# Half-size raw weight buffers, a fourth split buffer and five smaller moves in a two-layer encoder on one core

## The chip, the core and the metric

The kernel runs on one core of a Trainium2 chip. The metric is the time of one execution on the device in microseconds (us); the median of the timed runs counts. The core has a matrix engine (PE, with weight loads shown apart as PEld), a vector engine (DVE), a scalar engine (ACT), a general engine (POOL) and a queue engine that issues most DMAs (SP). Weights and activations come from HBM into an on-chip memory (SBUF); PE writes its sums into PSUM.

## The reference

An encoder of four sub-layers over 256 positions with 2048 channels, all in float32. Each is preceded by an RMS norm and added to the residual; a last RMS norm ends it.

```python
for i in range(DEPTH):                 # DEPTH = 2
    hn = rms_norm(h, mix_norm[i])
    h = h + (mixer_a(hn, ...) if i % 2 == 0 else mixer_b(hn, ...))
    h = h + conv_ffn(rms_norm(h, ffn_norm[i]), w_up[i], conv_w[i], conv_b[i], w_down[i])
return rms_norm(h, final_norm)
```

- Mixer A: attention with 16 query heads on 4 key and value heads of 128 channels. q and k are RMS-normalised per head, multiplied by a gain and rotated by row and column angles.
- Mixer B: three groups of 8 heads of dilated window attention with a table of relative biases; the groups are weighted by their softmax sums.
- FFN: an up-projection to 2 x 5632 channels, a width-3 convolution over positions for each channel (three taps and a bias per channel), then `silu(gate) * value`, then a down-projection.

## The kernel before

All 256 positions stay on the chip as the residual `h`; the weights stream past. A product of two float32 matrices is made of three matmuls in a reduced format: each operand is split into a high part (a rounded copy, made by ACT) and a low part (the rest, made by DVE), and high x high, high x low and low x high are added up in PSUM (`acc`).

**Weights.** `feed` handles a chunk of 512 x 512 weights (1 MB): one buffer `raw` (tag "raw", NRAW = 3), loaded by one DMA on SP, then two halves. For each half, ACT writes `wh` (line 150) and DVE writes `wl` (line 151), both of them tags with NHL = 3 buffers; then come 12 matmuls of 512 columns (lines 138 to 140). At the start of the kernel, where the hook loads the input beside the weights, a chunk is loaded in 4 or 2 pieces. `feed_T` is the same with the weights as the stationary operand, for the FFN's up-projection: one `raw` buffer holds two groups of 512 KB, each with its own DMA, split at lines 110 and 111, with 8 matmuls of 512 columns (line 122) and 8 of 256 (line 120).

**Order.** The program is written in order of use, and a scheduler fixes each engine's order when the kernel is built. Instructions under `tc.high_priority(offset=AHEAD)`, the splits of the weights, are ranked as if they stood 45 instructions earlier. An engine works through its queue in that fixed order and waits on semaphores.

**Work between the weights.** Everything that is not a weight matmul is a generator put into `pending` by `start`. `step()`, called after each half chunk, advances the first pending generator to its next `yield`; a generator that ends hands the same step to the next one. When nothing is pending, the step goes to `spare`, which holds the bias work. `step(True)`, in the middle of a half, only goes on after a `yield "half"`.

- `qk_post` (mixer A) scales and squares a projection, multiplies by cosines (DVE, line 583) and sines (POOL, line 588), reduces the squares (line 591), takes the root (DVE, then POOL at line 267, tile `rqk`) and adds the two products (line 594, tile `ro`). PE then transposes `ro` for q (`heads_T`, line 485).
- `attend` runs over the 4 heads of a group, six steps `k`: scores and exponentials of head `k`, transposition of head `k-1` (line 653) and product with v of head `k-2` (`mm3`, lines 204 to 206). Two heads share one PSUM tile `ot`. The result is split into the slots `ah` and `al` (lines 190 and 191). Four PSUM tiles (`psp`) serve all of this.
- `late_transpose` turns the new residual into the next layer's stationary operand by DVE block transposes (line 231) at the end of each sub-layer.
- `taps`, in `ffn`, transposes the convolution's taps (`cr`, loaded on POOL at lines 314 and 315) into `cw` by three PE transposes (line 322).
- `bias_lines`, the spare work of the first FFN, expands mixer B's bias table: one small matmul per block of four heads (line 692), a copy to `ln` (six buffers), and four DMAs on POOL to DRAM (line 698), from where mixer B reads skewed windows.

Of the kernel before, what the change touches and what calls it, by code (L numbers as in the profile page):

```python
# [13 lines left out]
P = 128  # L14
# [8 lines left out]
NRAW, NHL = 3, 3  # L23
AHEAD = 45
# [4 lines left out]
def tile_encoder(ctx: ExitStack, tc: tile.TileContext, x, xT, w_a, w_ao, q_gain, k_gain, w_b, w_bo,  # L29
# [68 lines left out]
    def feed_T(acc, lhs, w, n, hh, kgs, first, last):  # L98
        raw = spool.tile([P, 4, 512], F32, tag="raw", name=nm("raw"), bufs=NRAW)
        r = raw.rearrange("p a c -> p (a c)").rearrange("p (k c) -> p k c", c=NT)  # L100
        for i, kg in enumerate(kgs):
            src = w[n, kg].rearrange("p (k c) -> p k c", c=512)[:, :, hh * NT:(hh + 1) * NT]
            nc.sync.dma_start(r[:, 4 * i:4 * i + 4, :], src)
        for i, kg in enumerate(kgs):
# [3 lines left out]
            rk = r[:, 4 * i:4 * i + 4, :]  # L108
# [16 lines left out]
    def feed(accs, lhs, kg, wap, first, last, by_m=False, pieces=1, mid=None):  # L125
        raw = spool.tile([P, 4, 512], F32, tag="raw", name=nm("raw"), bufs=NRAW)
        rawf, w = raw.rearrange("p a c -> p (a c)"), 2048 // pieces
        for i in range(pieces):
            nc.sync.dma_start(rawf[:, i * w:(i + 1) * w], wap[:, i * w:(i + 1) * w])
            if mid is not None:  # L130
                mid(i)
        def mms(order):
            for m, kt in order:
                (wh, wl), j = hls[kt // 2], kt % 2
                xh, xl = lhs[4 * kg + kt][:2]
                st, sp = first and kt == 0, last and kt == 3
                c = slice(m * P, (m + 1) * P)
                nc.tensor.matmul(accs[m], xh[:, c], wh[:, j, :], start=st, stop=False)  # L138
                nc.tensor.matmul(accs[m], xh[:, c], wl[:, j, :], start=False, stop=False)  # L139
                nc.tensor.matmul(accs[m], xl[:, c], wh[:, j, :], start=False, stop=sp)  # L140
# [152 lines left out]
    def bcast_rstd(rbc, rstd, pool, more):  # L293
# [7 lines left out]
        more()  # L301

    def ffn(l, hT, ss_in, g_next, last, side=None):
        with tc.tile_pool(name=nm("fpool"), bufs=1) as fp:
# [7 lines left out]
            cr = fp.tile([P, 3, P], F32, name=nm("cr"))  # L312
            rows = conv[l].rearrange("b o (r c) -> (b o r) c", c=P)
            nc.gpsimd.dma_start(cr[:, 0:2, :], rows[0:2 * P].rearrange("(a p) c -> p a c", p=P))
            nc.gpsimd.dma_start(cr[:NROW - 2 * P, 2, :], rows[2 * P:NROW])
            cw = fp.tile([P, NROW], F32, name=nm("cw"))

            def taps():
                t = ps_tile()
                for a in range(3):  # L320
                    w = min(P, NROW - a * P)
                    nc.tensor.transpose(t[:, a * P:a * P + w], cr[:w, a, :], ident[:w, :w])
                nc.vector.tensor_copy(cw, t[:, :NROW])

# [9 lines left out]
            start(bcast_rstd(rbc, rstd, fp, taps))  # L334
# [166 lines left out]
    def mixer_a():  # L501
        with tc.tile_pool(name="apool", bufs=1) as ap:
# [4 lines left out]
            rp = ap.tile([P, 2, 2, P], F32, name="rp")  # L507
            gbs = [ap.tile([P, P], F32, name=f"gb{i}") for i in range(2)]
# [3 lines left out]
            def tables():  # L512
                nc.sync.dma_start(rp, rope)
                for (nme, g), gb in zip((("k", k_gain), ("q", q_gain)), gbs):
# [57 lines left out]
            def qk_post(accs, which, keep, scale=1.0):  # L572
# [10 lines left out]
                nc.vector.tensor_tensor(rv, sv, ct[:, :, None, :].to_broadcast([P, 2, 4, P]), ALU.mult)  # L583
# [6 lines left out]
                yield  # L590
                nc.vector.tensor_reduce(ssq, sq.rearrange("p m (a c) -> p (m a) c", a=4), axis=AX.X, op=ALU.add)
                rsqrt_mean(r, ssq, P * scale * scale, EPS / (scale * scale))
                yield
                nc.vector.tensor_tensor(ro, ro, t2, ALU.add)
# [18 lines left out]
            v = evac_split(ap, va, rstd[0])  # L613

            def attend(g, accs):
# [9 lines left out]
                for k in range(6):  # L625
# [31 lines left out]
                    if k >= 2:  # L657
                        i = k - 2
                        pT = pTs.pop(i)
                        if i % 2 == 0:  # L660
                            ot = ps_tile()
                        j = i % 2
                        for kt in range(2):
                            mm3(ot[:, j * NT:(j + 1) * NT], v, pT,
                                (slice(None), kt, slice(g * P, (g + 1) * P)),
                                (slice(None), slice(kt * NT, (kt + 1) * NT)), kt == 0, kt == 1)
                        hi, lo = slots[4 * g + i]
                        split(hi, lo, ot[:, j * NT:(j + 1) * NT])
# [3 lines left out]
            return out_proj(w_ao, slots, kgs, 1, 1, junk, ap, "sq")  # L672
# [4 lines left out]
    def bias_lines():  # L677
        with tc.tile_pool(name="lpool", bufs=1) as lp:
# [8 lines left out]
            for b in range(6):  # L687
# [6 lines left out]
                ln = lp.tile([P, 512], F32, tag="ln", name=nm("ln"), bufs=6)  # L694
                nc.vector.tensor_copy(ln[:, :w], t[:, :w])
                dst = scr0[4 * b:4 * b + 4] if b < 2 else scr1[4 * (b - 2):4 * (b - 2) + 4]
                for i in range(4):
                    nc.gpsimd.dma_start(dst[:, 32 * i:32 * i + 32, :], ln[:, :w])

    def mixer_b(hT, ss_in):  # L700
        with tc.tile_pool(name="bpool", bufs=1) as bp:
# [24 lines left out]

            allp = slice(None)
            for hf in range(2):
# [94 lines left out]
                for g in range(3):  # L823
# [7 lines left out]
            return out_proj(w_bo, slots, [0, 2, 4, 1, 3, 5], 3, 3, junk, bp, "vl")  # L831

    hT, ss = mixer_a()
    hT, ss = ffn(0, hT, ss, 2, False, bias_lines)
    hT, ss = mixer_b(hT, ss)
    ffn(1, hT, ss, None, True)

# [83 lines left out]
```

## Time and profile before

| | |
|---|---|
| timed runs | 2304.93, 2303.80, 2304.74 us; median 2304.74 |
| profiled execution | 2306.52 us, of which the span from first to last instruction is 2304.7 |
| granted PE clock | 0.999 of full speed |
| busy | PE 2286.8 us (99%), PEld 1945.6 (84%), DVE 1635.5 (71%), ACT 1220.0 (53%), POOL 168.5 (7%) |
| DMA | 437.50 MB, mean 190 GB/s |

How to read the rows of the profile. A group has the line, engine, operation, output tile and inputs, shapes and count, then busy time in us, mean duration of one in ns, and the engine's idle time before these instructions with what ended it. A row of the waits has "engine line <- who ended the wait: us in total, times, longest us". A row of the timeline has the start in us, the duration in us, engine, line, operation, tiles, count, and in brackets the idle time before it. A row of windows has the stretch, its length, the busy time of PE, PEld, DVE, ACT and POOL with the number of instructions, the granted PE clock, the share of the DMA engines and GB/s. A row of DMA issues has tiles, queue, count, size of one and the median time from issue to landing. PE's matmuls overlap and their ends are modelled, so their starts are what to compare.

### The profile page before, as it was taken

The page shows a single profiled execution, that of the slowest core. Times are in us where ns is not written, and L with a number is a line of the kernel's source. Part 1 is how long each engine was busy: PE and PEld are TensorE (multiplying, and loading weights), DVE is VectorE, ACT ScalarE, POOL GpSimd, SP SyncE. Part 2 cuts the span into 40 slices and gives each one's busy share as a digit, 9 for nine tenths or more (in the row PEclk, how much of TensorE's full clock was granted, in tenths as well). Part 3 has the DMA queues.
Part 4 walks back from the last instruction along what each step waited for, and adds up shares of the span by engine and source line. Part 5 has one row for each costly group of instructions (what it writes and reads, how often), then busy time and mean ns, then how long its engine had stood idle before and what let it go on. Part 6 is the DMA issues. An engine that isn't in the chain of part 4 may idle for free.

```text
span 2304.7 us, 30252 instructions
## 1 busy us (share of the span) xinstructions
PE 2286.8 (99%) x11641; PEld 1945.6 (84%) x11641; DVE 1635.5 (71%) x2285; ACT 1220.0 (53%) x1746; POOL 168.5 (7%) x167
## 2 busy tenths in 40 slices
PE   9999999999999999999999999999999999999998
PEld 7888788888888888888888888878888888888886
DVE  6877876776457776778876876576777754677755
ACT  6565565655345555445454454445556543555543
POOL 2331001200000000010000000000000000000010
PEclk9999999999999999999999999999999999999999
DMA  8434566755555555565555554556655555555654
GB/s 301 164 129 157 184 202 192 239 191 186 198 192 192 185 190 193 184 221 197 197 169 183 171 194 164 180 186 208 195 185 191 193 188 196 190 193 184 197 187 146
DMA packets 230337, 437.50 MB, mean 190 GB/s; under 512 B 13760, under 2 KB 194752, under 8 KB 202416
## 3 DMA queue, kind: packets, MB, share of 16 engines
q1 hardware_dynamic: 223808, 425.63, 55.0%
q0 software_dynamic: 5952, 9.38, 1.7%
q8 instruction: 91, 1.49, 0.3%
q10 hardware_dynamic: 432, 0.56, 0.1%
q14 instruction: 54, 0.44, 0.1%
HBM read 429.20 MB, written 6.29 MB: 189 GB/s over the span
## 4 chain that ended last, share of the span: by engine, by line
PE 90%; DVE 6%; DMA 1%; issue 1%; ACT 1%; SPq 0%; POOLq 0%; POOL 0%; DVEq 0%; ACTq 0%
PE acc L122 27%; PE acc L139 15%; PE acc L140 15%; PE acc L138 15%; PE acc L120 14%; DVE wl L151 2%; DVE tT L231 2%; DMA raw<-in_w_up_dram 1%; PE ps L202 1%; PE ps L204 0%; PE ps L205 0%; PE ps L206 0%; DVE h L285 0%; DMA xt<-in_xT_dram 0%; PE ps L799 0%
## 5 line engine op out<-in xcount | busy, mean ns | idle before, releaser
L151 DVE TENSOR_TENSOR wl<-raw,wh 128x1024 fp32r<-128x1024 f32 (+1 forms) x456 | 555.3, 1219 | 333.5 <-ACT wh L150 330.0
L150 ACT ACTIVATE wh<-raw 128x1024 fp32r<-128x1024 f32 (+1 forms) x456 | 475.3, 1045 | 527.1 <-PE acc L140 491.7
L122 PE MATMUL acc<-xh,wh 128*128 128x512 f32 x2816 | 675.3, 391 | 0.0
L122 PEld LDWEIGHTS acc<-xh,wh 128*128 128x128 f32 x2816 | 517.1, 188 | 101.0 <-issue 1.0
L111 DVE TENSOR_TENSOR wl<-raw,wh 128x1024 fp32r<-128x1024 f32 x352 | 457.9, 1301 | 192.2 <-ACT wh L110 191.9
L110 ACT ACTIVATE wh<-raw 128x1024 fp32r<-128x1024 f32 x352 | 372.5, 1059 | 211.8 <-PE acc L122 98.7
L139 PE MATMUL acc<-wl,ah 128*128 128x512 f32 x1024 | 400.0, 391 | 2.5 <-DVE wl L151 2.2
L138 PE MATMUL acc<-wh,ah 128*128 128x512 f32 x1024 | 399.2, 390 | 0.0
L140 PE MATMUL acc<-wh,al 128*128 128x512 f32 x1024 | 398.6, 389 | 0.0
L120 PEld LDWEIGHTS acc<-xh,wl 128*128 128x128 f32 x2816 | 361.6, 191 | 16.2 <-DVE wl L111 2.2
L120 PE MATMUL acc<-xh,wl 128*128 128x256 f32 x2816 | 366.6, 283 | 1.8 <-DVE wl L111 1.8
L138 PE MATMUL acc<-wh,xh 128*128 128x512 f32 x768 | 302.5, 395 | 0.3 <-ACT wh L150 0.2
L139 PE MATMUL acc<-wl,xh 128*128 128x512 f32 x768 | 299.8, 390 | 0.5 <-DVE wl L151 0.5
L140 PE MATMUL acc<-wh,xh 128*128 128x512 f32 x768 | 299.3, 390 | 0.0
L139 PEld LDWEIGHTS acc<-wl,ah 128*128 128x128 f32 x1024 | 192.2, 188 | 46.7 <-DVE wl L151 7.6
L138 PEld LDWEIGHTS acc<-wh,ah 128*128 128x128 f32 x1024 | 192.2, 188 | 39.8
L140 PEld LDWEIGHTS acc<-wh,al 128*128 128x128 f32 x1024 | 192.2, 188 | 39.6
L140 PEld LDWEIGHTS acc<-wh,xh 128*128 128x128 f32 x768 | 144.1, 188 | 30.2
L139 PEld LDWEIGHTS acc<-wl,xh 128*128 128x128 f32 x768 | 144.5, 188 | 29.3 <-DVE wl L151 1.7
L138 PEld LDWEIGHTS acc<-wh,xh 128*128 128x128 f32 x768 | 144.3, 188 | 28.6 <-ACT wh L150 1.2
L366 POOL TENSOR_TENSOR cv<-cg,cv 128x512 f32<-128x512 f32 x44 | 63.0, 1431 | 1137.8 <-DVE cv L358 1137.8
L346 ACT ACTIVATE v<-acc 128x256 f32<-128x256 f32 x176 | 66.4, 377 | 111.1 <-PE acc L122 111.1
(152 smaller groups left out, 1386.2 us busy)
## 6 DMA issues: line engine op xcount, KB each, us to landing
raw<-in_w_up_dram SPq DMA_DIRECT2D x352, 512.0 KB, 5.0
raw<-in_w_down_dram SPq DMA_DIRECT2D x88, 1024.0 KB, 4.8
raw<-in_w_b_dram SPq DMA_DIRECT2D x72, 1024.0 KB, 4.8
raw<-in_w_bo_dram SPq DMA_DIRECT2D x24, 1024.0 KB, 4.8
raw<-in_w_a_dram SPq DMA_DIRECT2D x16, 1024.0 KB, 4.8
raw<-in_w_ao_dram SPq DMA_DIRECT2D x16, 1024.0 KB, 4.8
raw<-in_w_a_dram SPq DMA_DIRECT2D x16, 256.0 KB, 5.8
raw<-in_w_a_dram SPq DMA_DIRECT2D x8, 512.0 KB, 8.7
```

The lines of the kernel that those rows point to most:

```text
L110: nc.scalar.activation(wh, rk, AF.Copy)
L111: nc.vector.tensor_tensor(wl, rk, wh.bitcast(F32), ALU.subtract)
L120: nc.tensor.matmul(acc[j][:, :NT], wl[:, kt, c], lhs[4 * kg + kt][0], start=st, stop=sp)
L122: nc.tensor.matmul(acc[j], wh[:, kt, c], lhs[4 * kg + kt][2], start=st, stop=sp)
L138: nc.tensor.matmul(accs[m], xh[:, c], wh[:, j, :], start=st, stop=False)
L139: nc.tensor.matmul(accs[m], xh[:, c], wl[:, j, :], start=False, stop=False)
L140: nc.tensor.matmul(accs[m], xl[:, c], wh[:, j, :], start=False, stop=sp)
L150: nc.scalar.activation(wh[:, c], r[:, c], AF.Copy)
L151: nc.vector.tensor_tensor(wl[:, c], r[:, c], wh[:, c].bitcast(F32), ALU.subtract)
L231: nc.vector.transpose(o[cols].rearrange("p a (m t) -> p a m t", m=2)[:, :, :, rows], s[rows].rearrange("p m (a c) -> p a m c", c=P)[:, :, ...
L346: nc.scalar.activation(v[:, j], acc[j][:, NT:], AF.Copy)
L366: nc.gpsimd.tensor_tensor(cv, cg, cv, ALU.mult)
```

## The change

- NRAW and NHL go from 3 to 4, AHEAD from 45 to 60. A `raw` buffer now holds half a chunk, so each half has its own buffer. In `feed` a chunk that one DMA of 1 MB loaded is loaded by two of 512 KB; in `feed_T` the two DMAs stay as they are.
- `load_taps` takes the loading and transposing of the taps out of `ffn`: mixer A calls it behind its v projection, mixer B at its start, and the transposes become a generator in the mixer's steps. `cr` and `cw` lie in the pool of the weights.
- `qk_post`: the product with the cosines moves one step later; the reduction and the root move behind the addition.
- `attend`: each head has its own PSUM tile for the product with v.
- `bias_lines`: a `yield` stands before each of the four DMAs, and `ln` has two buffers.
- The rotary tables `rp` and `gbs` share the buffers of the transposed probabilities, `pTh` and `pTl`.

```diff
-NRAW, NHL = 3, 3
-AHEAD = 45
+NRAW, NHL = 4, 4
+AHEAD = 60
...
     def feed_T(acc, lhs, w, n, hh, kgs, first, last):
-        raw = spool.tile([P, 4, 512], F32, tag="raw", name=nm("raw"), bufs=NRAW)
-        r = raw.rearrange("p a c -> p (a c)").rearrange("p (k c) -> p k c", c=NT)
-        for i, kg in enumerate(kgs):
+        raws = []
+        for kg in kgs:
+            raw = spool.tile([P, 2, 512], F32, tag="raw", name=nm("raw"), bufs=NRAW)
+            raws.append(raw.rearrange("p a c -> p (a c)").rearrange("p (k c) -> p k c", c=NT))
             src = w[n, kg].rearrange("p (k c) -> p k c", c=512)[:, :, hh * NT:(hh + 1) * NT]
-            nc.sync.dma_start(r[:, 4 * i:4 * i + 4, :], src)
+            nc.sync.dma_start(raws[-1], src)
...
     def feed(accs, lhs, kg, wap, first, last, by_m=False, pieces=1, mid=None):
-        raw = spool.tile([P, 4, 512], F32, tag="raw", name=nm("raw"), bufs=NRAW)
-        rawf, w = raw.rearrange("p a c -> p (a c)"), 2048 // pieces
-        for i in range(pieces):
-            nc.sync.dma_start(rawf[:, i * w:(i + 1) * w], wap[:, i * w:(i + 1) * w])
+        raws, w = [], 2048 // pieces
+        for i in range(max(pieces, 2)):
+            if pieces < 4 or i % 2 == 0:
+                raws.append(spool.tile([P, 2, 512], F32, tag="raw", name=nm("raw"), bufs=NRAW))
+            w = min(w, 1024)
+            r = raws[-1].rearrange("p a c -> p (a c)")
+            k = i % 2 if pieces == 4 else 0
+            nc.sync.dma_start(r[:, k * w:(k + 1) * w], wap[:, i * w:(i + 1) * w])
             if mid is not None:
                 mid(i)
...
-            r = raw[:, 2 * s:2 * s + 2, :]
+            r = raws[s]
...
+    def load_taps(l):
+        cr = spool.tile([P, 3, P], F32, tag="cr", name=nm("cr"), bufs=1)
+        cw = spool.tile([P, NROW], F32, tag="cw", name=nm("cw"), bufs=1)
+        rows = conv[l].rearrange("b o (r c) -> (b o r) c", c=P)
+        nc.gpsimd.dma_start(cr[:, 0:2, :], rows[0:2 * P].rearrange("(a p) c -> p a c", p=P))
+        nc.gpsimd.dma_start(cr[:NROW - 2 * P, 2, :], rows[2 * P:NROW])
+
+        def turn():
+            yield
+            t = ps_tile()
+            for a in range(3):
+                w = min(P, NROW - a * P)
+                nc.tensor.transpose(t[:, a * P:a * P + w], cr[:w, a, :], ident[:w, :w])
+            nc.vector.tensor_copy(cw, t[:, :NROW])
+
+        return cw, turn()
...
-            rp = ap.tile([P, 2, 2, P], F32, name="rp")
-            gbs = [ap.tile([P, P], F32, name=f"gb{i}") for i in range(2)]
+            rp = ap.tile([P, 2, 2, P], F32, tag="pTh", name="rp", bufs=2)
+            gbs = ap.tile([P, 4, P], F32, tag="pTl", name="gbs", bufs=2)
...
             def qk_post(accs, which, keep, scale=1.0):
...
-                nc.vector.tensor_tensor(rv, sv, ct[:, :, None, :].to_broadcast([P, 2, 4, P]), ALU.mult)
...
                 yield
+                nc.vector.tensor_tensor(rv, sv, ct[:, :, None, :].to_broadcast([P, 2, 4, P]), ALU.mult)
+                yield
+                nc.vector.tensor_tensor(ro, ro, t2, ALU.add)
                 nc.vector.tensor_reduce(ssq, sq.rearrange("p m (a c) -> p (m a) c", a=4), axis=AX.X, op=ALU.add)
                 rsqrt_mean(r, ssq, P * scale * scale, EPS / (scale * scale))
-                yield
-                nc.vector.tensor_tensor(ro, ro, t2, ALU.add)
...
             v = evac_split(ap, va, rstd[0])
+            cw, turn = load_taps(0)
+            start(turn)
...
-                        if i % 2 == 0:
-                            ot = ps_tile()
-                        j = i % 2
+                        ot = ps_tile()[:, :NT]
...
-                ln = lp.tile([P, 512], F32, tag="ln", name=nm("ln"), bufs=6)
+                ln = lp.tile([P, 512], F32, tag="ln", name=nm("ln"), bufs=2)
...
                 for i in range(4):
+                    yield
                     nc.gpsimd.dma_start(dst[:, 32 * i:32 * i + 32, :], ln[:, :w])
...
     def mixer_b(hT, ss_in):
...
+            cw, turn = load_taps(1)
...
+                if hf == 0:
+                    start(turn)
                 for g in range(3):
                     start(v_gen(g, project(w_b, 6 * g + 4 + hf, hT, kgs)))
```

More of the change, by code (lines that the diff above doesn't have):

```diff
@@ L291, in junk_of, with bcast_rstd @@
         return lambda: pool.tile([P, 512], F32, tag="junk", name=nm("junk"))
-    def bcast_rstd(rbc, rstd, pool, more):
+    def bcast_rstd(rbc, rstd, pool):
         dg = pool.tile([P, 2, P], F32, name=nm("dg"))
@@ L300, in bcast_rstd, with ffn @@
         nc.vector.tensor_copy(rbc, t[:, :NT])
-        more()
-    def ffn(l, hT, ss_in, g_next, last, side=None):
+    def load_taps(l):
[12 more added lines that the diff above has]
+        return cw, turn()
+    def ffn(l, hT, ss_in, cw, g_next, last, side=None):
         with tc.tile_pool(name=nm("fpool"), bufs=1) as fp:
@@ L311, in ffn @@
                 nc.gpsimd.dma_start(fin, final_norm.partition_broadcast(P))
[L312 to L323, printed above, removed]
             def tap(n, j, i):
@@ L333, in ffn @@
             rb4 = rbc.rearrange("p (m t) -> p m t", m=2)[:, None].to_broadcast([P, 2, 2, P])
-            start(bcast_rstd(rbc, rstd, fp, taps))
+            start(bcast_rstd(rbc, rstd, fp))
             def halves(v):
@@ L513, in tables @@
                 nc.sync.dma_start(rp, rope)
-                for (nme, g), gb in zip((("k", k_gain), ("q", q_gain)), gbs):
+                for i, (nme, g) in enumerate((("k", k_gain), ("q", q_gain))):
+                    gb = gbs[:, i, :]
                     nc.sync.dma_start(gb, g.partition_broadcast(P))
```

19 lines of the change are left out of this document (9 added, 10 removed).

## The prediction

> **What bounds the kernel now.** I read the page first, then the waits of PE's weight loads over the whole run, then the timelines of PE, DVE and ACT around each wait found there.
>
> ```profile
> span 2304.7 us, 30252 instructions
> PE 2286.8 (99%) x11641; PEld 1945.6 (84%) x11641; DVE 1635.5 (71%) x2285; ACT 1220.0 (53%) x1746; POOL 168.5 (7%) x167
> PEld acc L139 <- DVE wl L151: 9.2, 15, 0.9
> PEld ps L204 <- DVE al L191: 2.8, 3, 0.9
> PEld acc L120 <- DVE wl L111: 2.2, 1, 2.2
> PEld ps L485 <- DVE ro L594: 1.4, 1, 1.4
> ```
>
> PE is busy 99% of the span and nearly always has its operands. The change removes no large matmul, so it can only win back the moments at which PE stood still. These are few: 15 waits for the low half `wl` of a split weight in `feed`, 3 for a low half `al` in mixer A, 1 for `wl` in `feed_T`, 1 for the rotated query `ro`. The change touches each of them. A microsecond taken out of PE's stream comes off the end, since no other engine is near its limit (DVE 71%).
>
> PEld's idle time overstates a stall, because a load normally runs ahead of its matmul. The loss is the spacing of matmul starts against the steady one:
>
> ```profile
> 257.30 0.39 PE L140 MATMUL acc<-wh,al 128*128 128x512 f32 x1
> 257.52 0.39 PE L138 MATMUL acc<-wh,ah 128*128 128x512 f32 x1
> 258.42 0.50 PE L139 MATMUL acc<-wl,ah 128*128 128x512 f32 x1 [0.51 <-DVE wl L151]
> 258.76 0.40 PE L140 MATMUL acc<-wh,al 128*128 128x512 f32 x1
> ```
>
> Steady spacing is 0.23 us (257.30 to 257.52; over long stretches 0.227). Here it is 0.90 and then 0.34, so the wait cost 0.67 + 0.11 = 0.78 us, 0.15 less than the 0.93 us that PEld idled. I take 0.15 off each PEld wait. A half chunk of `feed` is 12 such matmuls, 12 x 0.227 = 2.72 us; that is the beat of the kernel.
>
> **Fourth split buffer and AHEAD.** Where do the 15 waits lie? The same view in three stretches (230 to 270, 960 to 1000, 1500 to 1520 us), which are the ends of mixer A, of the first FFN and of mixer B, and DVE's timeline in the first:
>
> ```profile
> PEld acc L139 <- DVE wl L151: 3.7, 6, 0.9
> PEld acc L139 <- DVE wl L151: 1.8, 3, 0.8
> PEld acc L139 <- DVE wl L151: 2.0, 3, 0.9
> 254.88 2.23 DVE L231 STREAM_TRANSPOSE tT<-h 32x256 f32<-32x256 f32 x5
> 257.14 1.23 DVE L151 TENSOR_TENSOR wl<-raw,wh 128x1024 fp32r<-128x1024 f32 x1
> 230.00:270.00 40.00, 38.80 (x167) 30.22 (x167) 38.17 (x63) 21.35 (x33) 0.00 (x0) 1.00 0.48 162
> ```
>
> Twelve waits, 7.5 us less 12 x 0.15, so 5.7 us of PE time. The cause is seen in DVE: five block transposes of the next layer's input stand before each split, 2.23 + 1.23 = 3.46 us of DVE work to a beat of 2.72, so DVE falls 0.7 us behind with each half until the block is done. Over the whole stretch it keeps up (38.17 us of 40). With three buffers a `wh` may be written once PE has finished the half three back; with four, one beat (2.72 us) earlier. The stretches lose 2.8 (in two groups 15 us apart), 1.35 and 1.55 us, each less than the beat gained. I count 5.2 of the 5.7 us, bounds 3.0 (DVE's fixed order puts some split still later) and 5.7. The other three waits (1.7 us of PEld, 1.25 after the deduction) lie in the first 20 us, where data, not buffers, are late: 0, at best 1.25.
>
> **Raw half chunks.** The four half-size buffers hold four halves where three whole ones held six, but a half is now freed by its own `wl` and not by its partner's.
>
> ```profile
> raw<-in_w_up_dram SPq DMA_DIRECT2D x352, 512.0 KB, 5.0
> raw<-in_w_down_dram SPq DMA_DIRECT2D x88, 1024.0 KB, 4.8
> raw<-in_w_a_dram SPq DMA_DIRECT2D x8, 512.0 KB, 8.7
> L151 DVE TENSOR_TENSOR wl<-raw,wh 128x1024 fp32r<-128x1024 f32 (+1 forms) x456 | 555.3, 1219 | 333.5 <-ACT wh L150 330.0
> L150 ACT ACTIVATE wh<-raw 128x1024 fp32r<-128x1024 f32 (+1 forms) x456 | 475.3, 1045 | 527.1 <-PE acc L140 491.7
> 800.00:810.00 10.00, 10.00 (x61) 8.92 (x60) 6.71 (x11) 5.77 (x8) 0.00 (x0) 1.00 0.66 208
> ```
>
> A slot's round is landing + `wh` + `wl` = 5.0 + 1.05 + 1.22 = 7.3 us against 4 beats = 10.9 us, so 3.6 us hide the smaller store. Each 1024 KB transfer becomes two of 512 KB; on SP only weights stand behind them. No trace has such a half transfer in this place: the nearest rows are 5.0 us (same size, 1 KB rows) and 8.7 us (same rows as the new ones, but in the first 40 us, where the queues are full). Cost 0 at 5.0; a round at 8.7 is 10.97 us, just the limit.
>
> The Trainium skill ("DMA: Bandwidth & Descriptors", section Bandwidth) says to batch transfers to 1 MiB or more for 75% of peak, which speaks against halving them. Its formula in the section on the anatomy of one DMA (2.0 us + bytes / 436 GB/s, given for GpSimd's path) makes 3.2 us of 512 KB, an estimate, more than a beat if they came one at a time. The trace disagrees: the last row is a stretch of `feed_T`, which already lives on 512 KB transfers, and PE is busy 10.00 of 10.00 us at 208 GB/s.
>
> At the start the store matters, because the fourth chunk's pieces are issued early:
>
> ```profile
> 11.71 2.59 SPq L129 DMA_DIRECT2D raw<-in_w_a_dram  x4
> 14.48 1.28 DVE L151 TENSOR_TENSOR wl<-raw,wh 128x512 fp32r<-128x512 f32 x2
> 15.00:20.00 5.00, 4.73 (x21) 3.62 (x20) 4.49 (x8) 4.59 (x9) 0.00 (x0) 1.00 1.03 401
> ```
>
> They will have to wait for the second chunk's splits, the last of which ends at 15.8, so up to 2.5 us later, with the loads of x and the rotary tables behind them on SP. But the DMA engines are full there (share 1.03): a transfer that joins a full queue later, in the same order, lands hardly later. Bounds 0 and +1.5, I take +0.6.
>
> **PSUM tile per head.**
>
> ```profile
> 108.62 0.39 PE L139 MATMUL acc<-wl,xh 128*128 128x512 f32 x1
> 109.53 0.39 PE L204 MATMUL ps<-pTh,vh 128*128 128x256 f32 x1 [0.52 <-DVE al L191]
> 109.76 0.28 PE L205 MATMUL ps<-pTl,vh 128*128 128x256 f32 x1
> 109.88 0.28 PE L206 MATMUL ps<-pTh,vl 128*128 128x256 f32 x1
> 108.47 0.68 DVE L191 TENSOR_TENSOR pTl<-ps,pTh 128x512 fp32r<-128x512 f32 x1
> 109.07 0.41 DVE L191 TENSOR_TENSOR al<-ps,ah 128x256 fp32r<-128x256 f32 x1
> ```
>
> The fourth head's product waits for `al` of the third, which is read from the other half of the same tile. Loss 0.91 - 0.23, and 0.23 - 0.12 after it: 0.79 us, in three of the four groups, 2.4 us. With a tile of its own the product can start at 108.85. Next late is `pTl` (done at 109.15), which its second matmul needs at 108.97: up to 0.35 us stays if DVE's queue is as before, so at least 1.3 us is won; DVE has less before it (next part), so I take 2.2. A step now takes three of the four tiles, and a score tile gets the slot of a product two steps older, some 5 us: free, and 0.8 us a time where that cover fails.
>
> **Rotary of q and k.**
>
> ```profile
> 81.27 0.39 PE L140 MATMUL acc<-wh,xh 128*128 128x512 f32 x1
> 82.68 1.09 PE L485 MATMUL ps<-ident,ro 128*128 128x128 f32 x8 [1.02 <-DVE ro L594]
> 80.29 1.20 DVE L591 TENSOR_REDUCE ssq<-sq 128x8 f32<-128x1024 f32 x1
> 81.42 1.21 DVE L594 TENSOR_TENSOR ro<-ro,t 128x1024 f32<-128x1024 f32 x1
> 53.08 2.56 POOL L267 TENSOR_TENSOR rqk<-ms,nhalf 128x8 f32<-128x8 f32 x1 [1.82 <-DVE ms L266]
> ```
>
> PE lost 1.41 - 0.23 = 1.18 us here. With the reduction behind the addition, `ro` ends 1.2 us earlier, at about 81.5, when PE wants it. The multiplication by the cosines moves one beat later, in front of it; I take 1.0, bounds 0 and 1.2. The root `rqk` for q starts when it does now, since reduction and addition only change places. For k the root comes up to one beat and one reduction (1.20) later, 3.9 us, and DVE would stand before the product with it, at worst for all of that, with the splits behind it. The fourth buffer covers 2.72 of the 3.9 us: 0.2 lost, bounds 0 and 1.2.
>
> **Bias copies.**
>
> ```profile
> 402.11 0.59 PE L692 MATMUL ps<-oh,lh 128*128 128x256 f32 x2
> 404.46 1.21 PE L120 MATMUL acc<-xh,wl 128*128 128x256 f32 x8 [1.76 <-DVE wl L111]
> raw<-in_w_up_dram SPq DMA_DIRECT2D x10, 512.0 KB, 11.4
> scr<-ln POOLq DMA_DIRECT2D x8, 256.0 KB, 16.8
> ```
>
> The last two rows are the transfers between 376 and 410 us: copies of four at a time, up to 1 MB, and beside them weights that need 11.4 instead of 5.0 us. PE pays once: the starts of L692 and L120 are 2.35 us apart, of which the row counts 1.76 as idle; some 2.0 us can go. One copy per spare step (some five spare steps in eight `feed_T` beats of 2.8 us, one in 4.4 us) adds 58 GB/s instead of a burst, so I take 1.9, bounds 1.0 (some delay stays) and 2.0. `ln` with two buffers waits for copies eight or more spare steps old, 35 us against the 16.8 us of landing: free.
>
> **Taps, tables in other tiles.** The three transposes and one copy are moved, not removed; PE does not wait at the old place nor need it at the new one; the two small transfers go ahead on POOL, busy 7%. 0.
>
> **Sum.** 5.2 + 2.2 + 1.0 + 1.9 - 0.6 - 0.2 = 9.5 us. The profiled execution took 2306.52 us (span 2304.7 and 1.8 around it), so 2297.0 for such a one; the median of the three timed runs is 2304.74, 0.08% less, and the forecast is 2304.7 - 9.5 = 2295.2. All bounds at their best: 5.7 + 1.25 + 2.4 + 1.2 + 2.0 = 12.6, 2292.2. All at their worst: 3.0 + 1.3 + 0 + 1.0 - 1.5 - 1.2 = 2.6, 2302.1.
>
> **Rivals.**
> A. *The fourth buffer does not help*: the order of DVE's queue is fixed, and transposes keep their places before the splits. Against: DVE has 1.8 us in 40 to spare, and each loss is under a beat. For: a longer AHEAD moves the order in ways that this trace cannot show. Without its 5.2 us: 2300.4.
> B. *Slower: splits in front of evacuations.* ACT works in order and already spends 491.7 us in front of a `wh`, waiting for PE. If the fourth buffer and the longer AHEAD put one more `wh` ahead of the exponentials and evacuations of mixer A, then PE waits for these at a price like that of `al`, 0.79. At all 32 places (16 heads, transposition and product) 25 us: 2304.7 - 9.5 + 25 = 2320. It turns the sign from 12 places on. Against: the waits end with the same PE events as now.
> C. *Slower: half transfers too slow.* Should a half take 9.6 us (two transfers of 4.8 one behind the other), a round is 11.9 us, 0.24 us per half over the beat: for the 176 halves of `w_down` alone 42 us, 2337. It begins at 8.6 us of landing. The batching rule of the Trainium skill ("DMA: Bandwidth & Descriptors", section Bandwidth) would lead here. `feed_T` speaks against it.
> D. *Given back in the rotary*: if DVE stands 1.5 us before the root in k and in each of four q groups with the splits behind it, 7.5 us return: 2302.7.
>
> **Chances.** Forecast 0.70, A 0.10, D 0.08, B 0.08, C 0.04. The measurement can tell 0.2%, 4.6 us, from no change: faster means under 2300.1. The forecast is faster but for its worst corner (0.68), A is on the line (0.05 each side), D is the same, B and C slower: 0.73, 0.15, 0.12. A range of 2292 to 2303 holds the forecast, A and D.
>
> **What would show it.** Right: PEld's waits for `wl` of `feed` fall from 15 to the few of the first 20 us; those for `al`, for `wl` of `feed_T` and for `ro` vanish; PE stays at 99%; landing of the 512 KB halves under 8 us. Wrong: PE waits on `wh` with a DMA as releaser (C), on `pTh` or `ah` in mixer A (B), on `wl` at the same three stretches (A), or DVE idles before L607 or L636 with POOL as releaser (D).

## The result and the profile after

| | before | after |
|---|---|---|
| median of 8 timed runs (lowest to highest), us | 2304.73 (2303.80 to 2305.41) | 2298.35 (2297.71 to 2299.45) |
| profiled execution, us (span) | 2306.52 (2304.7) | 2298.31 (2296.5) |

The ratio is 0.9971, with a 95% interval of 0.9962 to 0.998: the change makes the kernel faster by 6.4 us, 0.28%. The forecast was 2295.2 us, range 2292 to 2303. The time alone does not decide for the forecast: it is 3.2 us from it and 2.1 us from the 2300.4 of rival A, both of which the range holds. Note the profiled execution of before: it lies 1.8 us above the median of its kind, while that of after lies on its median. That difference matters below.

Span and busy times from the page of the kernel after:

```profile
span 2296.5 us, 31097 instructions
PE 2283.0 (99%) x11641; PEld 1947.3 (85%) x11641; DVE 1633.6 (71%) x2285; ACT 1218.4 (53%) x1746; POOL 164.7 (7%) x167
```

Those of PEld's waits over the whole run that bear on the change, after (L144 was L138 before, L145 was L139, L121 was L120, L123 was L122, L494 was L485):

```profile
PEld acc L123 <- DVE v L356: 1.9, 3, 1.4
PEld acc L144 <- ACT wh L156: 1.6, 1, 1.6
PEld ps L494 <- DVE ro L602: 1.0, 1, 1.0
PEld acc L145 <- DVE wl L157: 0.8, 2, 0.5
PEld acc L121 <- DVE wl L112: 0.7, 2, 0.4
```

Of the 15 waits for `wl` of `feed` 2 are left, both in the first 20 us; the three stretches at the ends of the sub-layers have none left. The waits for `al` are gone, and no `pTl` came in their place. `ro` is waited for 1.0 instead of 1.4 us. The wait for `wh` at the start is 1.6 us once, where before had 1.2 us in two. The wait for `v` (L356), an evacuation in the FFN, is new.

The spacing of PE's starts turns this into time:

| place | lost before, us | lost after, us |
|---|---|---|
| `wl` at the three sub-layer ends | 2.82 + 1.35 + 1.57 = 5.74 | 0 |
| `al`, three groups | 3 x 0.79 = 2.36 | 0 |
| `ro` at 81 us | 1.18 | 0.75 |
| bias work near 402 us | 2.0 in the profiled execution | 0 |
| first 20 us | 4.0 | 4.0 |
| start of the first FFN, 279 to 288 us | 0 | 2.2 |

Without the bias row that is 5.74 + 2.36 + 0.43 - 2.2 = 6.3 us, the 6.4 of the medians.

The last row of the table is what the prediction did not have. After, DVE's timeline at the first FFN's start, and those of DVE and PE some 9 us later:

```profile
270.45 0.48 DVE L302 TENSOR_SCALAR dg<-ident,rstd 128x128 f32<-128x128 f32 x2 [0.61 <-POOL rstd L273]
276.65 0.56 DVE L695 COPY lh<-rb 128x768 f32<-128x768 f32 x1 [5.71 <-DMA rb<-in_rel_bias_dram]
```

```profile
285.91 0.42 DVE L356 TENSOR_TENSOR v<-acc,v 128x256 f32<-128x256 f32 x1
286.38 1.23 DVE L112 TENSOR_TENSOR wl<-raw,wh 128x1024 fp32r<-128x1024 f32 x1
287.52 0.75 DVE L356 TENSOR_TENSOR v<-acc,v 128x256 f32<-128x256 f32 x2
284.54 2.34 PE L123 MATMUL acc<-xh,wh 128*128 128x512 f32 x9
287.99 1.88 PE L123 MATMUL acc<-xh,wh 128*128 128x512 f32 x7 [1.11 <-DVE v L356]
```

`lh` belongs to the spare bias work and is not wanted before the bias blocks near 370 us. Its copy stands in DVE's queue, waiting for a load `rb` of 3 KB, and for 5.71 us nothing passes it: the splits and `v` are late, and PE pays 0.37 us and some tenths from 279 us on, then 1.38 + 0.11 at 286.4. Before, the same copy, which ran only 0.65 us later, cost nothing, since two splits and an `xh` were queued ahead of it:

```profile
272.80 1.22 DVE L111 TENSOR_TENSOR wl<-raw,wh 128x1024 fp32r<-128x1024 f32 x1
274.22 1.23 DVE L111 TENSOR_TENSOR wl<-raw,wh 128x1024 fp32r<-128x1024 f32 x1 [0.20 <-ACT wh L110]
275.36 0.48 DVE L197 SCALAR_TENSOR_TENSOR xh<-ps,gain,xh 128x256 fp32r<-128x256 f32 x1
277.30 0.56 DVE L686 COPY lh<-rb 128x768 f32<-128x768 f32 x1 [1.46 <-DMA rb<-in_rel_bias_dram]
```

The landing of the weights after, on which rival C of the prediction turns:

```profile
raw<-in_w_up_dram SPq DMA_DIRECT2D x352, 512.0 KB, 3.8
raw<-in_w_down_dram SPq DMA_DIRECT2D x176, 512.0 KB, 3.7
```

### The profile page after: what moved, and what is told of

The parts are those of the page before. It is cut to its first block, busy times and chain, and to the rows that moved or that the text cites. A ratio compares the mean times of both kernels' runs of the same rounds, so it can differ in the third digit from the quotient of the medians.

```text
span 2296.5 us, 31097 instructions
## 1 busy us (share of the span) xinstructions
PE 2283.0 (99%) x11641; PEld 1947.3 (85%) x11641; DVE 1633.6 (71%) x2285; ACT 1218.4 (53%) x1746; POOL 164.7 (7%) x167
## 3 DMA queue, kind: packets, MB, share of 16 engines
q8 instruction: 91, 1.49, 0.3%
## 4 chain that ended last, share of the span: by engine, by line
PE 94%; DVE 3%; issue 1%; DMA 1%; POOL 0%; ACT 0%; SPq 0%; POOLq 0%; DVEq 0%; ACTq 0%
PE acc L123 27%; PE acc L145 16%; PE acc L144 16%; PE acc L146 16%; PE acc L121 14%; DVE tT L237 1%; DVE wl L157 1%; PE ps L208 1%; PE ps L211 1%; PE ps L210 0%; PE ps L212 0%; DMA raw<-in_w_a_dram 0%; PE ps L665 0%; PE ps L810 0%; DMA rb<-in_rel_bias_dram 0%
## 5 line engine op out<-in xcount | busy, mean ns | idle before, releaser
L123 PE MATMUL acc<-xh,wh 128*128 128x512 f32 x2816 | 675.5, 391 | 1.1 <-DVE v L356 1.1
L123 PEld LDWEIGHTS acc<-xh,wh 128*128 128x128 f32 x2816 | 517.1, 188 | 102.1 <-DVE v L356 1.9
L144 PE MATMUL acc<-wh,ah 128*128 128x512 f32 x1024 | 399.1, 390 | 0.0
L145 PE MATMUL acc<-wl,ah 128*128 128x512 f32 x1024 | 398.5, 389 | 0.0
L121 PEld LDWEIGHTS acc<-xh,wl 128*128 128x128 f32 x2816 | 361.9, 191 | 15.4 <-DVE wl L112 0.7
L121 PE MATMUL acc<-xh,wl 128*128 128x256 f32 x2816 | 367.8, 283 | 0.2 <-DVE wl L112 0.2
L144 PE MATMUL acc<-wh,xh 128*128 128x512 f32 x768 | 302.5, 395 | 1.2 <-ACT wh L156 1.2
L145 PE MATMUL acc<-wl,xh 128*128 128x512 f32 x768 | 299.9, 391 | 0.2 <-DVE wl L157 0.2
L144 PEld LDWEIGHTS acc<-wh,ah 128*128 128x128 f32 x1024 | 192.3, 188 | 39.3
L145 PEld LDWEIGHTS acc<-wl,ah 128*128 128x128 f32 x1024 | 192.2, 188 | 39.2
L144 PEld LDWEIGHTS acc<-wh,xh 128*128 128x128 f32 x768 | 144.4, 188 | 29.4 <-ACT wh L156 1.6
L145 PEld LDWEIGHTS acc<-wl,xh 128*128 128x128 f32 x768 | 144.3, 188 | 27.9 <-DVE wl L157 0.8
```

The source lines that it names most:

```text
L121: nc.tensor.matmul(acc[j][:, :NT], wl[:, kt, c], lhs[4 * kg + kt][0], start=st, stop=sp)
L123: nc.tensor.matmul(acc[j], wh[:, kt, c], lhs[4 * kg + kt][2], start=st, stop=sp)
```

## Experiments

Each time below stands beside the kernel before on the same chip: 2304.48 us for p_buffers, p_heads, p_bias and f_lh, 2304.52 for p_bufheads, p_buftaps, u_nhl3 and f_lhrot, 2304.27 for p_half, p_rot, u_ahead45 and f_lhrotlate.

### One part of the change at a time

**p_buffers**: before, with the buffers and AHEAD alone.

```diff
-NRAW, NHL = 3, 3
-AHEAD = 45
+NRAW, NHL = 4, 4
+AHEAD = 60
...
```

(`feed` and `feed_T` are those of the change.)

> The kernel before with the half-size raw buffers, the fourth split buffer and AHEAD 60 alone. Theory (each stall is its own and the gains add): the twelve waits for wl at the three sub-layer ends go, 5.7 us, so 2299.0 against 2304.7; PEld's waits for wl of feed fall from 15 to the 3 of the start; the waits for al (3), ro (1) and the bias stall of feed_T stay. Rival (the gain of the whole change comes from the small edits, and halved transfers cost what the buffers win): 2303 to 2306.

2301.47 us (2300.00 to 2304.54), ratio 0.9985 [0.9976, 0.9993]. The `wl` waits at the sub-layer ends are gone, but only 3.0 us are won, since a new wait took 3.7 back. PEld's two longest waits:

```profile
PEld ps L210 <- DVE al L197: 3.1, 3, 1.1
PEld ps L328 <- DMA cr<-in_conv_dram: 2.8, 3, 1.3
```

PE's timeline at the second of them:

```profile
274.17 0.44 PE L328 MATMUL ps<-ident,cr 128*128 128x128 f32 x2 [0.89 <-DMA cr<-in_conv_dram]
275.48 0.30 PE L328 MATMUL ps<-ident,cr 96*128 96x96 f32 x1 [0.87 <-DMA cr<-in_conv_dram]
```

Two windows behind it, in which the column after the five engines is the granted clock:

```profile
274.50:278.00 3.50, 2.63 (x14) 2.23 (x14) 0.58 (x2) 0.84 (x2) 0.00 (x0) 0.82 0.97 339
278.00:282.00 4.00, 4.00 (x15) 3.20 (x15) 3.67 (x8) 1.42 (x2) 0.00 (x0) 0.73 0.54 172
```

With PE earlier at the FFN's start, the taps `cr` come too late for their transposes: 1.15 + 1.04 us. Then the granted clock falls (0.82 and 0.73 of full speed in the windows): eight matmuls follow at up to 0.43 instead of 0.23 us, 1.5 us more.

The wait for `ro`, which was expected to stay, is gone too, although the rotary steps are those of before. DVE's timeline:

```profile
80.00 1.22 DVE L600 TENSOR_TENSOR ro<-ro,t 128x1024 f32<-128x1024 f32 x1
```

The addition ends at 81.2 us, in time for PE; before it ended at 82.6. With these 1.2 us the sum closes: 5.7 + 1.2 - 3.7 = 3.2. The half-size buffers alone do not do it, since p_half below keeps the wait.

**p_heads**: before, with a PSUM tile per head alone.

```diff
-                        if i % 2 == 0:
-                            ot = ps_tile()
+                        ot = ps_tile()[:, :NT]
```

> The kernel before with a PSUM tile per head alone. Theory: the three waits for al go whole, 2.4 us, 2302.3. Rival (pTl is next late, the rotary work still stands before it on DVE): PE waits at the second matmul of the fourth head, 1.3 us gained, 2303.4, and three waits for pTl appear at L205.

2304.07 us, ratio 1.0 [0.9991, 1.0009]: nothing. PE's timeline and DVE's in the first of the three groups:

```profile
108.09 0.28 PE L204 MATMUL ps<-pTh,vh 128*128 128x256 f32 x1
108.89 0.38 PE L205 MATMUL ps<-pTl,vh 128*128 128x256 f32 x1 [0.53 <-DVE pTl L191]
106.89 1.34 DVE L151 TENSOR_TENSOR wl<-raw,wh 128x1024 fp32r<-128x1024 f32 x1
108.16 0.68 DVE L191 TENSOR_TENSOR pTl<-ps,pTh 128x512 fp32r<-128x512 f32 x1
```

The product now starts at once and stops one matmul later, for `pTl`: 0.80 - 0.12 + 0.10 = 0.78 us, as much as `al` had cost. `pTl` stands behind a split. And PE's own order has changed: 12 matmuls of `acc` stand between this product and the one before it, where before there were 14. So PE reaches the product 0.45 us earlier, and the 0.35 us that the prediction left at `pTl` become 0.8.

**p_bias**: before, with the bias copies alone.

```diff
-ln = lp.tile([P, 512], F32, tag="ln", name=nm("ln"), bufs=6)
+ln = lp.tile([P, 512], F32, tag="ln", name=nm("ln"), bufs=2)
...
                 for i in range(4):
+                    yield
                     nc.gpsimd.dma_start(dst[:, 32 * i:32 * i + 32, :], ln[:, :w])
```

> The kernel before with one bias copy per spare step and two ln buffers alone. Theory: the 2.0 us stall of feed_T near 402 us is in every execution, so 2302.7. Rival (that stall was a feature of the one profiled execution, which at 2306.5 was 1.8 us above the median of the timed runs): 2304.4 to 2304.9, though the profile shows no such stall.

2304.18 us, ratio 0.9997 [0.9988, 1.0006]. The stall at 402 us is not in its profile, but the time is that of before. Nor is it in the profiles of p_heads (span 2302.3), p_rot, p_buffers, p_bufheads and p_buftaps, all of which have the bias copies of before. So the 2.0 us belonged to the one execution of before that was profiled, the one 1.8 us above the median.

**p_rot**: before, with the rotary steps alone.

```diff
-                nc.vector.tensor_tensor(rv, sv, ct[:, :, None, :].to_broadcast([P, 2, 4, P]), ALU.mult)
...
                 yield
-                nc.vector.tensor_reduce(ssq, ...)
-                rsqrt_mean(r, ssq, ...)
+                nc.vector.tensor_tensor(rv, sv, ct[:, :, None, :].to_broadcast([P, 2, 4, P]), ALU.mult)
                 yield
                 nc.vector.tensor_tensor(ro, ro, t2, ALU.add)
+                nc.vector.tensor_reduce(ssq, ...)
+                rsqrt_mean(r, ssq, ...)
```

> The kernel before with the rotary steps alone: the cosine product one step later, the addition in the third step ahead of the reduction. Theory of the prediction: the addition ends 1.2 us earlier, the wait of 1.18 us at 81 us goes, and the later root of k costs 0.2 to 1.2 with only three split buffers: 2303.7, bounds 2303.3 to 2304.7. Rival: it changes the order on DVE in the query groups as well, so that the product or the split of a score stands behind a split or an addition there, three times or more, 2306 or over.

2304.14 us, ratio 1.0 [0.9991, 1.0009]. PEld's waits between 60 and 100 us:

```profile
PEld acc L139 <- DVE wl L151: 0.8, 1, 0.8
PEld ps L485 <- DVE ro L592: 0.3, 1, 0.3
```

DVE's timeline:

```profile
80.72 1.21 DVE L592 TENSOR_TENSOR ro<-ro,t 128x1024 f32<-128x1024 f32 x1
81.86 1.20 DVE L593 TENSOR_REDUCE ssq<-sq 128x8 f32<-128x1024 f32 x1
```

Here the addition does stand ahead of the reduction, and the stall of 1.18 us is gone. For k a wait for a split at 70.3 us gives 0.58 + 0.11 = 0.69 us back, inside the prediction's bound of 0 to 1.2. Another 0.26 us is lost at 86 us, where the scores wait for `qTl`. The loss in k is of the kind of rival D, work of `qk_post` that holds up the splits, but DVE does not stand before the root: it stands 0.63 us before the addition, waiting for POOL's product `t`:

```profile
51.00 1.23 DVE L592 TENSOR_TENSOR ro<-ro,t 128x1024 f32<-128x1024 f32 x1 [0.63 <-POOL t L587]
```

**p_half**: before, with half-size raw buffers alone.

```diff
-NRAW, NHL = 3, 3
+NRAW, NHL = 4, 3
...
```

(`feed` and `feed_T` are those of the change; AHEAD stays 45.)

> The kernel before with half-size raw buffers (four of 512 KB in place of three of 1 MB), three split buffers and AHEAD 45 left as they are. Theory: the smaller store is hidden (a slot's round of 3.7 + 1.05 + 1.22 = 6.0 us against four beats, 10.9 us), so 2304.5 us within 2 us, the twelve wl waits at the sub-layer ends still there. Rival: the half transfers cost time by themselves, part of what the changed kernel with three split buffers lost (17.9 us over the changed kernel, 11.7 over the one before): then 2308 to 2316, with PE waiting for wh or wl with a DMA behind it.

2307.14 us (2305.41 to 2312.31), ratio 1.0014 [1.0005, 1.0023]: slower by 2.9 us, where I expected nothing within 2. The profiled execution (2306.41 us) has the stalls of before, with PE's loss 1.3 us larger than in that of p_bias: 0.5 us of it at `ro`, 0.4 near 397 us, 0.2 for the taps of the second FFN. The rest of the 2.9 us was not located.

### Parts together

**p_bufheads**: p_buffers and p_heads in one.

```diff
-NRAW, NHL = 3, 3
-AHEAD = 45
+NRAW, NHL = 4, 4
+AHEAD = 60
...
-                        if i % 2 == 0:
-                            ot = ps_tile()
+                        ot = ps_tile()[:, :NT]
```

> The kernel before with the buffers (half-size raw, fourth split, AHEAD 60) and the PSUM tile per head. Theory: the tile per head alone only changed what PE waits for (from al to pTl, which stands behind a split on DVE); with the fourth buffer pTl is ordered one split earlier, so together they win the 2.4 us that neither wins alone: 2299.1 against the 2301.5 of the buffers alone, no wait for al nor pTl. Rival (the rotary edit is what cleared DVE): PE waits for pTl three times as before, 2301.5.

2297.19 us (2296.58 to 2299.52), ratio 0.997 [0.9959, 0.9981]. PEld's waits for `cr` and `wl`:

```profile
PEld ps L328 <- DMA cr<-in_conv_dram: 3.4, 3, 1.7
PEld acc L145 <- DVE wl L157: 2.0, 4, 0.6
```

Neither `al` nor `pTl` is there. The PSUM tile, worth nothing alone, takes 4.3 us off p_buffers by the medians (whose runs spread over 4.5 us) and 2.3 us between the two profiled spans (2300.0, 2297.7); the stalls for `al` that it removes from p_buffers come to 2.7. The reason stands in DVE's timeline, where `pTl` is now ahead of the split, as it already is in p_buffers:

```profile
106.08 0.68 DVE L197 TENSOR_TENSOR pTl<-ps,pTh 128x512 fp32r<-128x512 f32 x1
106.67 1.43 DVE L157 TENSOR_TENSOR wl<-raw,wh 128x1024 fp32r<-128x1024 f32 x1
```

The profiled execution here is the slowest of its seven, 2.3 us above the median, and holds the wait for `cr` and a slow clock behind it, so that this wait need not be in every execution.

These two parts alone are 7.3 us under before, the whole change 6.4, and the intervals overlap. That the other parts of the change (rotary steps, taps, tables, bias copies) win anything on top of them is not shown.

**p_buftaps**: p_buffers with the taps loaded and transposed in the mixers, and the tables in the buffers of `pTh` and `pTl`, without which it does not fit into SBUF.

```diff
+            cw, turn = load_taps(0)
+            start(turn)
...
-            rp = ap.tile([P, 2, 2, P], F32, name="rp")
+            rp = ap.tile([P, 2, 2, P], F32, tag="pTh", name="rp", bufs=2)
...
```

> The kernel before with the buffers, the taps made in the mixers and the rotary tables in other tiles (without which it doesn't fit into the memory). Theory: with the buffers alone PE came to the taps' transposes before their data and lost 2.2 us of waiting and 1.6 us at half clock; with the taps made ready earlier this 3.8 us goes, but DVE's wait for the small bias table takes 2.3 us in its place: 2299.5 to 2300 against 2301.5. Rival (the wait for the taps was a matter of one execution): 2301.5 or more.

2300.56 us (2299.63 to 2302.57), ratio 0.998 [0.9972, 0.9989]. The wait for `cr` and the slow clock behind it (3.7 us) are gone; only 0.9 us of it shows in the medians and 2.1 in the profiled spans (2300.0, 2297.9). Part came back at the same place: `lh` now stands in DVE's queue without splits ahead of it, as DVE's timeline shows, and PE loses 1.4 us at 287.6.

```profile
277.78 0.56 DVE L698 COPY lh<-rb 128x768 f32<-128x768 f32 x1 [4.86 <-DMA rb<-in_rel_bias_dram]
```

### After with one thing changed

**f_lh**: the copy of `lh` on POOL instead of DVE.

```diff
-            nc.vector.tensor_copy(lh, rb[:, :, None].to_broadcast([P, 24, 32]))
+            nc.gpsimd.tensor_copy(lh, rb[:, :, None].to_broadcast([P, 24, 32]))
```

> The changed kernel with the copy of the bias table into lh moved from DVE to POOL. Theory: DVE's 5.7 us wait for a 3 KB transfer at the start of the first FFN is what makes PE stand for some 2.3 us between 279 and 288 us; both go, 2296.0 against 2298.35. Rival (these stalls come from the four half-size raw buffers, which hold less in front of feed_T): DVE's wait goes, PE's stalls stay, 2298.3.

2296.78 us (2295.87 to 2297.40), ratio 0.9963 [0.995, 0.9975]: 7.7 us under before, against 6.4 for after. In its profile the stalls of 279 to 288 us are gone, and its span is 2.4 us shorter than that of after (2294.1, 2296.5). Of that the medians show 1.3, with overlapping intervals; the profiled execution is 0.9 us below its median.

**u_nhl3**: three split buffers.

```diff
-NRAW, NHL = 4, 4
+NRAW, NHL = 4, 3
```

> The changed kernel with three split buffers instead of four, all else as changed. Theory (the fourth buffer, not the half-size raw ones, removes the twelve waits for wl): the waits come back, 5.7 us, and pTl stands behind a split again, 2.4 us: about 2306. Rival (half-size raw buffers and AHEAD do it): 2298 to 2299.

2316.22 us (2314.23 to 2318.15), ratio 1.005 [1.0038, 1.0063]: 11.7 us slower than before, 18 slower than after. The `wl` waits are back (8.4 us in 14); that explains the expected part. The rest lies in mixer A. The timelines of DVE and PE there:

```profile
108.27 1.23 DVE L602 TENSOR_TENSOR ro<-ro,t 128x1024 f32<-128x1024 f32 x1 [2.03 <-POOL t L597]
109.41 1.22 DVE L157 TENSOR_TENSOR wl<-raw,wh 128x1024 fp32r<-128x1024 f32 x1
110.55 0.69 DVE L197 TENSOR_TENSOR pTl<-ps,pTh 128x512 fp32r<-128x512 f32 x1
108.48 0.28 PE L210 MATMUL ps<-pTh,vh 128*128 128x256 f32 x1
111.29 0.39 PE L211 MATMUL ps<-pTl,vh 128*128 128x256 f32 x1 [2.53 <-DVE pTl L197]
```

Three windows, one behind each such stall:

```profile
112.20:115.60 3.40, 3.40 (x9) 2.65 (x8) 2.13 (x5) 1.32 (x2) 1.16 (x1) 0.50 0.79 241
146.35:149.70 3.35, 3.35 (x11) 2.87 (x12) 2.88 (x5) 0.38 (x1) 0.00 (x0) 0.50 0.89 215
182.00:186.00 4.00, 4.00 (x19) 3.20 (x19) 3.40 (x6) 1.44 (x2) 1.64 (x1) 1.00 0.69 232
```

The number of buffers has changed DVE's order. The addition `ro`, which nobody wants for a long while, stands ahead of `pTl` and waits 2.03 us for POOL's product (in after `pTl` starts at 106.95 and the addition at 110.71); PE waits for `pTl` 2.7 us in each of three groups. After two of them the clock is granted at half (0.50) for 3.4 us and costs another 1.6 us each time. These are 11.3 us; with the 5.7 of the `wl` waits, 17.0 of the 18.

**u_ahead45**: AHEAD back at 45, four buffers kept.

```diff
-AHEAD = 60
+AHEAD = 45
```

> The changed kernel with AHEAD 45 instead of 60, four split buffers kept. Theory: the gain at the sub-layer ends is the buffer's and not the longer priority offset's, so no wl waits come back at 240 to 270, 968 to 995 and 1509 to 1516 us: 2298.3 within 1.5 us; the two kernels differ mainly in where reductions and splits stand on DVE in mixer A, which may move the wait for ro by 0.5 us. Rival: the offset carries part of it, wl waits of 2 us or more come back, 2300.5 or over.

2295.80 us (2295.26 to 2297.23), ratio 0.9963 [0.995, 0.9976]: 8.5 us under before. No `wl` wait comes back at the sub-layer ends, so the gain there is the buffer's. Against after the longer AHEAD costs 2.1 us (6.4 and 8.5 under their befores). DVE's timeline at two places:

```profile
78.46 1.33 DVE L157 TENSOR_TENSOR wl<-raw,wh 128x1024 fp32r<-128x1024 f32 x1
79.71 1.21 DVE L602 TENSOR_TENSOR ro<-ro,t 128x1024 f32<-128x1024 f32 x1
276.83 0.56 DVE L695 COPY lh<-rb 128x768 f32<-128x768 f32 x1 [6.04 <-DMA rb<-in_rel_bias_dram]
286.05 0.75 DVE L356 TENSOR_TENSOR v<-acc,v 128x256 f32<-128x256 f32 x2
```

One split stands ahead of `ro` instead of two, and `ro` is in time; `lh` waits as long as ever, but the two pieces of `v` follow each other without a split between them, and PE does not stop there. That is 0.75 + 1.38 = 2.1 us, what the medians say. The profiled spans differ by only 1.0 us (2296.5, 2295.5): the profiled execution of u_ahead45 is the slowest of its five, 1.4 us above the median, and loses 0.7 us more than that of after in the first 20 us.

**f_lhrot**: `lh` on POOL, and the addition raised by 20 places.

```diff
+                with tc.high_priority(offset=20):
-                nc.vector.tensor_tensor(ro, ro, t2, ALU.add)
+                    nc.vector.tensor_tensor(ro, ro, t2, ALU.add)
```

> The changed kernel with lh copied on POOL and the rotary addition ranked 20 places earlier, so that it stands between two splits and behind the reduction. Theory: the addition can begin when POOL ends the sine products, some 1.0 us earlier for the first group, so the 0.75 us that PE still loses before the first q transposes goes: 2296.0 against the 2296.8 with lh alone. Rival (DVE then waits for POOL in front of a split, and in the later groups in front of pTl): 2296.8 to 2299, with waits for wl or pTl in mixer A.

2295.25 us (2294.89 to 2295.70), ratio 0.996 [0.9947, 0.9972]: 9.3 us under before, the lowest of all, though u_ahead45 is within its interval. The stall at 81 us is gone; DVE's timeline shows the addition starting as soon as POOL's product `t` allows:

```profile
80.11 1.23 DVE L603 TENSOR_TENSOR ro<-ro,t 128x1024 f32<-128x1024 f32 x1 [0.64 <-POOL t L597]
```

**f_lhrotlate**: the same, with the taps' loads held back until `v` exists.

```diff
-            cw, turn = load_taps(0)
+            cw, turn = load_taps(0, v[0][:, 0, 0:1].bitcast(F32))
...
-    def load_taps(l):
+    def load_taps(l, after=None):
...
+        if after is not None:
+            for a in (0, 2):
+                nc.gpsimd.tensor_copy(cr[:, a, 0:1], after)
```

> The changed kernel with lh copied on POOL, the rotary addition put ahead of the reduction, and the taps' two loads for the first FFN held back until v exists, so that they and their three transposes no longer stand in the first 10 us. Theory: the start loses the wait for wh near 7 us (0.7 to 1.4 us in the profiles of the changed kernel and of the version without the hold), so 0.5 to 1.0 us under that version's 2295.25: 2294.5. Rival: the start waits for x and the weights, which arrive when they arrive, and the taps (180 KB) are no part of it: 2295.3 within 0.4.

2296.48 us (2296.03 to 2297.76), ratio 0.9966 [0.9953, 0.9979]. PEld's wait for `ro`:

```profile
PEld ps L497 <- DVE ro L606: 0.9, 1, 0.9
```

Neither theory gave this time (2294.5 and 2295.3 were expected). The rival was right in that the start waits on without the taps: by the spacing of its starts PE loses 3.6 us in the first 20 us, 4.0 in f_lhrot, so the taps are at most a small part of what is late there. The wait for `ro` is back: the addition starts at 80.80, 0.7 us later than in f_lhrot. Why POOL's product is later stays open.

## Why the prediction was right, and where its terms were off

The direction, the range and the main mechanism held; the forecast was 3.2 us too low. Of the signs that it named, the waits for `wl` of `feed` and for `al` and the landing of the halves came as said; the wait for `ro` did not vanish, and `wl` of `feed_T` is waited for at another place. By the terms of its sum:

- **Fourth split buffer, 5.2 (bounds 3.0 to 5.7): 5.74.** All twelve waits went, and u_nhl3 and u_ahead45 show that the buffer does it and not AHEAD. Rival A is out.
- **PSUM tile, 2.2: 2.36.** Right as a size, and `pTl` was rightly named as next late. But the bound of 1.3 "if DVE's queue is as before" was wrong: with that queue p_heads won nothing. The bound took PE's order as fixed, and in p_heads the product stands two matmuls earlier, so that `pTl` is late by as much as `al` was. The tile pays where `pTl` stands ahead of the split, as it does with the new buffers (p_bufheads).
- **Rotary, 1.0: 0.43.** The step that failed is "with the reduction behind the addition". The program says so, DVE's queue doesn't: the scheduler put the reduction first, then two splits. That it did so because the reduction's input is ready earlier is argued only. DVE after:

```profile
77.09 1.21 DVE L603 TENSOR_REDUCE ssq<-sq 128x8 f32<-128x1024 f32 x1
78.22 3.02 DVE L157 TENSOR_TENSOR wl<-raw,wh 128x1024 fp32r<-128x1024 f32 x2
81.17 1.21 DVE L602 TENSOR_TENSOR ro<-ro,t 128x1024 f32<-128x1024 f32 x1
```

Nor are the 0.43 us shown to be a gain of these steps: p_buffers, p_bufheads and p_buftaps have the new buffers and the rotary steps of before, and in none of them does PE wait for `ro`. So the buffers with AHEAD win the 1.18 us by themselves, and in after, with the steps moved, 0.75 of it is lost again; no run takes these steps alone out of after.

- **Root of k, -0.2: 0** with four buffers; 0.69 with three and AHEAD 45 (p_rot). With three and AHEAD 60 PE loses 0.1 us there (u_nhl3), so that it is the fourth buffer that covers, as the prediction had it, is not shown.
- **Bias copies, 1.9: 0.** The largest error. The stall was real in one execution and no part of the median. The prediction subtracted it from the median, though the profiled execution was itself 1.8 us above; a term that stands in the excess has to be taken from the excess.
- **Start, -0.6: 0.** PE's loss in the first 20 us is 4.0 us in both profiles, differently spread.
- **Taps, 0: wrong in both directions.** "PE does not wait at the old place" was true of before alone: with the buffers PE arrives earlier and does wait there (p_buffers, 3.7 us), so the move keeps a gain that would be lost, 0.9 us of it by the medians of p_buftaps. And with the two DMAs and the transposes gone from the FFN's start, `lh` stands in front there (p_buftaps, where p_buffers has two splits and an `xh` ahead of it): -2.2 us, which go when the copy goes to POOL (f_lh). That the copy moved up because POOL issues `rb` earlier (270.6 instead of 273.8 us) is argued only.
- **Raw half chunks, 0: not settled.** The sum below closes without a term for them, but alone they cost 2.9 us, of which 1.3 were found as stalls in its profile (p_half).

In sum 9.5 - 1.9 (bias) - 0.6 (rotary) - 2.2 (`lh`) + 0.55 + 0.15 + 0.6 + 0.2 = 6.3. Rival C is out: halves land in 3.7 to 3.8 us where 8.6 was the limit. Batching to 1 MiB, by the Trainium skill ("DMA: Bandwidth & Descriptors", section Bandwidth), is not refuted by that: halving alone was 2.9 us slower (p_half), in part for reasons not located. Rival B, at 0.08, did not decide the sign, but something like it is in this change, on DVE and in the FFN instead of on ACT in mixer A: after has a split between two evacuations at 286.4 us (1.49 us), and u_nhl3 shows with `ro` in place of a split how dear a wrong order is. Rival D did not come with four buffers.

## What to carry to other kernels

Before a stall is counted as a gain, see whether the profiled execution lies above the median by about as much; if it does, the stall may belong to that execution alone. Where a scheduler fixes an engine's order, the order of the program is no evidence: each edit, a number of buffers too, must be read in the new queue, above all for low-priority work that waits for a load and for evacuations that stand behind splits. Parts of a change need not add up: one may be worth nothing alone (the PSUM tile), only guard what another wins (the taps), or aim at a wait that another has already removed (the rotary steps).

## What the runs showed of the hardware

A stall of PE of under 3 us can cost more than itself. In u_nhl3 three equal gaps of 2.8 us between matmul starts came 35 us apart. After the first, eight matmuls of 512 columns ran at 0.43 us each; after the second, five such and four of 256 columns at 0.21; after the third none was slow (granted clock 0.50, 0.50 and 1.00 in the windows behind them). In p_buffers two gaps, 1.15 and 1.04 us over the steady spacing and within 2.6 us, had the same result: eight slow matmuls. The gap of 2.1 us between two starts in before, at 402 us, had not: the granted clock stayed at 1.00. The Trainium skill ("TensorE: Matmul & The Clock Gate", section What's actually happening) explains it by a free-running window of 3.4 us; the eight slow matmuls last 8 x 0.43 = 3.4 us, which agrees, and that only two of three equal gaps had an effect fits a window that runs free, while gaps of 2.8 us, shorter than the window, sufficed here.
